# A prefix log-sum-exp: stores on ScalarE's DMA ring, loads on SyncE's, and the last tile in the common stream

## The chip, the cores and the metric

The kernel runs on one core of a Trainium2 chip. The metric is the device time of one execution in microseconds (us): the median of nine runs, and beside it the span and the trace of one profiled execution. Five engines work side by side, each through its own list of instructions in order: TensorE (PE; PEld for its weight loads), VectorE (DVE), ScalarE (ACT), GpSimd (POOL) and SyncE (SP). Transfers between the main memory (DRAM) and the on-chip buffer are done by 16 DMA engines; SyncE or ScalarE issue them with an instruction that returns at once, and a semaphore tells when the transfer has landed.

## The reference

For each batch and each of the 4128 columns, the running log of the sum of exponentials along the 4096 rows:

```python
B, S, D = (4, 4096, 4128)          # x: float32, normal draws
out[:, 0, :] = x[:, 0, :].copy()
for t in range(1, S):
    mx = np.maximum(out[:, t - 1, :], x[:, t, :])
    out[:, t, :] = mx + np.log(np.exp(out[:, t - 1, :] - mx) + np.exp(x[:, t, :] - mx))
```

That is out[t] = log(exp(x[0]) + ... + exp(x[t])), a prefix sum between an exponential and a logarithm. Input and output are 270.5 MB each, so 541 MB have to be moved.

## The kernel before

**Tiles.** The rows of a batch are cut into steps (class `Step`) of 384 rows, three to each of the 128 partitions, which lie one behind the other in DRAM: a partition's share of a full step is one stretch of 3 x 4128 x 4 = 49536 bytes. Ten such steps and one of 256 rows (33024 bytes to a partition) make a batch. In the first batch the short step comes first, in the other three last. So there are 44 steps, numbered 0 to 43; step 0 and step 43 are short. A step's tile `xt` is loaded by one DMA, worked on in place, and stored by one DMA. The pool `xpool` has four buffers (`bufs`).

**Chunks.** A step is worked on in four chunks of columns (class `Chunk`), in the order 3, 0, 1, 2 (`order`); chunk 3 (`firstc`) has 1056 columns, the others 1024. For each chunk: `act(Exp)` on ScalarE; `own` on VectorE adds the partition's own rows, the total going to `tot`; `head` on TensorE puts into PSUM (`above`) the sum of all the partitions above, by a matrix multiplication with a triangle of ones, and for chunk 2 the carry from the step before; `add_above` on VectorE adds that to the rows, and for chunk 2 copies the carry out; `complete` on TensorE leaves the step's total in PSUM for the next step; `act(Ln)` on ScalarE ends it. The last 32 columns of chunk 3 have a small sequence of their own (`tail_head`, `carry_t`).

**The order.** It is written out by hand (`tc.manual_schedule`, lines 196 to 213), and the framework only adds the semaphores. In round g of the loop come: Exp of chunk g+2, `own` and `head` of chunk g+1, `add_above` and `complete` of chunk g, and `result` of chunk g-1, which is its Ln and, behind a step's last chunk (2), the store. So on ScalarE, Exp of three chunks of a step stand ahead of the last Ln of the step before. The loop of line 196 runs twice: over steps 0 to 42 together, and then over step 43 alone, so that the stream of rounds drains between the two.

**The queues.** All loads and stores are issued by SyncE (lines 103 and 106), in program order. The first four loads are issued at the start. Then, in `result`, the store of step k is issued, and right behind it the load of step k+3 (`ahead` is 3; the condition of line 191 begins with step 4). That load goes into the buffer of step k-1, and so it waits until the store of step k-1 has landed. A store waits for the last Ln of its step. As SyncE's list is in order, a waiting store also holds back the load that stands behind it. All transfers go through one queue of the DMA engines (q1 in the profile), as a ring from which each engine takes packets in order: a transfer gives each of the 16 engines 8 packets, one for each of 8 partitions, and a four-byte semaphore write behind them.

**Names in the profile.** L118 is every Exp and Ln (`Chunk.act`), L86 every add, L83 every matrix multiplication, L155 the copies of the carry, L103 a load, L106 a store.

Of the kernel before, what the change touches and what calls it, by code (L numbers as in the profile page):

```python
# [9 lines left out]
ACT = mybir.ActivationFunctionType  # L10
# [28 lines left out]
def kernel(  # L39
# [14 lines left out]
    nc = tc.nc  # L54
# [5 lines left out]
    order = [NC - 1] + list(range(NC - 1))  # L60
    firstc, lastc = order[0], order[-1]
# [5 lines left out]
    bufs = 4  # L67
# [20 lines left out]
    class Step:  # L88
# [14 lines left out]
            nc.sync.dma_start(out=self.xt, in_=self.dram(x))  # L103

        def store(self):
            nc.sync.dma_start(out=self.dram(out), in_=self.xt)  # L106

    class Chunk:
        def __init__(self, step, c):
# [58 lines left out]
    steps = []  # L168
# [9 lines left out]
            row += P * r  # L178
        assert row == S

    ahead = bufs - 1
    for s in steps[:bufs]:
        s.load()
    stored = 0

    def result(k):
        nonlocal stored
        k.act(ACT.Ln)
        if k.c == lastc:
            k.t.store()  # L190
            if bufs <= stored + ahead < len(steps):
                steps[stored + ahead].load()
            stored += 1


    for part in (steps[:-1], steps[-1:]):
        chunks = [Chunk(s, c) for s in part for c in order]
        N = len(chunks)
        for g in range(-2, N + 1):
            if 0 <= g + 2 < N:  # L200
                chunks[g + 2].act(ACT.Exp)
            if 0 <= g + 1 < N:
                chunks[g + 1].own()
                chunks[g + 1].head()
            if 0 <= g < N:
                chunks[g].add_above()
                if g + 1 < N and chunks[g + 1].c == firstc:
                    chunks[g + 1].tail_head()
                chunks[g].complete()
            elif g == -1:  # L210
                chunks[0].tail_head()
            if 0 <= g - 1:
                result(chunks[g - 1])


# [28 lines left out]
```

The softmax here doesn't subtract the row's maximum and nothing guards it: scores larger than these inputs give would overflow.

## Time and profile before

| what | time, us |
|---|---|
| median of nine runs (lowest to highest) | 1265.2 (1264.2 to 1266.37) |
| the profiled execution | 1264.2 |
| its span, from the first to the last instruction | 1262.4 |
| ScalarE (ACT), busy of the span | 921.0 |
| VectorE (DVE), busy of the span | 1024.2 |
| ScalarE waiting for loads, 41 times | 314.9 |
| a full load, from issue to landing (median of 40) | 41.9 |
| a full store, from issue to landing (median of 40) | 27.7 |
| the store of the last step, from issue to landing | 11.1 |

Columns of the views that follow: a timeline's line is start, duration, engine, source line, operation, output and input, number of instructions merged, and in brackets the idle time ahead of it and what ended it. A line of the windows' table is a stretch of time, its length, then busy time and number of instructions by engine, the clock granted to TensorE, the mean busy share of the 16 DMA engines, and what these moved in GB/s. A packet is counted whole in the window in which it starts, so that a share can come out a little over 1. The line of a queue gives its packets, its megabytes, and the time of its packets as a share of 16 engines' span. The trace also holds a record of each packet (start, duration, size, queue, but not which of the 16 engines) and of each engine's share in each landing.

### The profile page before, as it was taken

What the parts mean: (1) busy time and instruction counts of PE and PEld (TensorE: products, weight loads), DVE (VectorE), ACT (ScalarE), POOL (GpSimd) and SP (SyncE); (2) the same over time, 40 slices, a digit from 0 to 9 for tenths busy, and PEclk for the clock granted to TensorE, in tenths of its full rate; (3) what the DMA queues carried; (4) which work ended last, traced back from release to release, by engine and by line L of the source; (5) the groups of instructions that cost most, each with busy time, mean ns of one, the idle gap of its engine ahead of it and who ended that gap; (6) DMA issues with size and microseconds to landing.
All of it is one profiled execution on the core that took longest, in us unless ns stands there. A gap on an engine that the chain in (4) does not pass through costs nothing.

```text
span 1262.4 us, 3545 instructions
## 1 busy us (share of the span) xinstructions
PE 484.1 (38%) x876; PEld 221.4 (18%) x876; DVE 1024.2 (81%) x858; ACT 921.0 (73%) x353; POOL 1.5 (0%) x10
## 2 busy tenths in 40 slices
PE   2445433343334434443324434443332443443332
PEld 1212111111111112211111112211111211111111
DVE  4999878888888888888679888887867988887784
ACT  4986677777777776668669776666966977666784
POOL 0000000000000000000000000000000000000000
PEclk9865656555565555556556565555555656555556
DMA  9999999999999999999999999999999999999997
GB/s 410 413 444 424 427 430 441 432 430 437 432 432 430 440 432 429 433 438 434 435 431 431 432 440 433 427 433 438 426 425 435 429 438 432 433 430 437 435 403 340
DMA packets 12692, 541.29 MB, mean 429 GB/s; under 512 B 1408, under 2 KB 1408, under 8 KB 1408
## 3 DMA queue, kind: packets, MB, share of 16 engines
q1 hardware_dynamic: 12672, 541.07, 99.4%
q8 instruction: 7, 0.11, 0.0%
q14 instruction: 13, 0.11, 0.0%
HBM read 270.53 MB, written 270.53 MB: 429 GB/s over the span
## 4 chain that ended last, share of the span: by engine, by line
DMA 69%; ACT 19%; issue 7%; DVE 3%; SPq 0%; PE 0%; DVEq 0%; ACTq 0%
DMA xt<-in_x_dram 63%; ACT xt L118 19%; DMA out_dram<-xt 6%; DVE xt L86 3%; DVE tot L86 1%; SPq L106 0%; PE above L83 0%; DVE carry L155 0%; DVEq L239 0%; ACTq L118 0%; DVE carry_t L155 0%; DVEq L86 0%
## 5 line engine op out<-in xcount | busy, mean ns | idle before, releaser
L118 ACT ACTIVATE xt<-xt 128x3072 f32<-128x3072 f32 (+3 forms) x352 | 919.7, 2692 | 328.6 <-DMA xt<-in_x_dram 314.9
L83 PE MATMUL above<-tot,excl 128*128 128x512 f32 (+1 forms) x396 | 257.4, 719 | 476.5 <-DVE tot L86 472.2
L86 DVE TENSOR_TENSOR xt<-xt,above 128x2048 f32<-128x2048 f32 (+3 forms) x220 | 393.3, 1788 | 0.0
L86 DVE TENSOR_TENSOR xt<-xt 128x1024 f32<-128x1024 f32 (+1 forms) x160 | 196.9, 1231 | 179.9 <-ACT xt L118 177.5
L86 DVE TENSOR_TENSOR tot<-xt 128x1024 fp32r<-128x1024 f32 (+1 forms) x176 | 217.0, 1233 | 40.5 <-ACT xt L118 18.9
L86 DVE TENSOR_TENSOR xt<-tot,above 128x1024 f32<-128x1024 f32 (+1 forms) x220 | 221.3, 1006 | 0.0
L83 PEld LDWEIGHTS above<-tot,excl 128*128 128x128 f32 x396 | 104.8, 306 | 607.7 <-DVE tot L86 566.5
L83 PE MATMUL above<-tot,rest 128*128 128x512 f32 x240 | 129.5, 635 | 201.8 <-DVE xt L86 201.8
L83 PE MATMUL above<-carry,pick 128*128 128x512 f32 x160 | 141.9, 987 | 0.0
L83 PEld LDWEIGHTS above<-tot,rest 128*128 128x128 f32 x240 | 53.3, 277 | 294.3 <-DVE xt L86 292.5
L83 PE MATMUL above<-carry_t,pick 128*128 128x32 f32 x80 | 25.2, 409 | 83.2 <-DVE xt L86 83.2
L83 PEld LDWEIGHTS above<-carry,pick 128*128 128x128 f32 x160 | 52.0, 325 | 11.3
L83 PEld LDWEIGHTS above<-carry_t,pick 128*128 128x128 f32 x80 | 20.2, 312 | 110.3 <-DVE xt L86 108.3
L155 DVE COPY carry<-xt 32x1024 f32<-32x1024 f32 x40 | 27.6, 691 | 1.4
L155 DVE COPY carry_t<-xt 32x32 f32<-32x32 f32 x40 | 7.1, 177 | 1.4
L63 ACT ACT_TABLE_LOAD x1 | 1.3, 1283 | 0.8 <-PEq L228 0.8
L77 DVE MEMSET carry<- 128x1024 f32 x1 | 0.9, 912 | 1.1 <-PEq L228 1.1
L24 POOL TENSOR_SCALAR_AFFINE_SELECT excl<-excl 128x128 fp32r<-128x128 f32 x1 | 0.3, 293 | 0.0
L24 POOL TENSOR_SCALAR_AFFINE_SELECT pick<-pick 128x128 f32<-128x128 f32 x1 | 0.3, 292 | 0.1
L24 POOL TENSOR_SCALAR_AFFINE_SELECT rest<-rest 128x128 fp32r<-128x128 f32 x1 | 0.3, 292 | 0.0
L23 POOL MEMSET pick<- 128x128 f32 x1 | 0.2, 205 | 0.0
L23 POOL MEMSET excl<- 128x128 f32 x1 | 0.2, 204 | 0.3 <-POOLq L228 0.3
(6 smaller groups left out, 0.7 us busy)
## 6 DMA issues: line engine op xcount, KB each, us to landing
xt<-in_x_dram SPq DMA_DIRECT2D x40, 6192.0 KB, 41.9
out_dram<-xt SPq DMA_DIRECT2D x40, 6192.0 KB, 27.7
xt<-in_x_dram SPq DMA_DIRECT2D x4, 4128.0 KB, 37.0
out_dram<-xt SPq DMA_DIRECT2D x4, 4128.0 KB, 25.4
```

Of the source, the lines that this page charges most:

```text
L23: nc.gpsimd.memset(t.bitcast(FP32), 1.0 - fill)
L24: nc.gpsimd.affine_select(out=t, in_=t, pattern=[[step, P]], compare_op=op, fill=fill, base=base, channel_multiplier=-step if step else 1,)
L63: nc.scalar.preload_act_table_set("natural_log_exp_and_others")
L77: nc.vector.memset(carry, 0.0)
L83: nc.tensor.matmul(o, lhsT=w, rhs=rhs, start=start, stop=True, skip_group_check=True)
L86: nc.vector.tensor_tensor(out=o, in0=a, in1=b, op=mybir.AluOpType.add)
L118: nc.scalar.activation(v, v, func)
L155: nc.vector.tensor_copy(cr[96:, :], t.xt[96:, n, a:b])
```

## The change

Stores are issued by ScalarE, so that they go through a ring of their own. They stand in ScalarE's list right behind the step's last Ln. SyncE's list holds nothing but loads: behind the first four, the load of step k+4 is written behind the store of step k, into the buffer of that same step, and waits until that store has landed. The loop over two parts is gone: step 43 runs in one stream with the steps before it. On ScalarE, three Exp of step 43 now stand ahead of the last Ln of step 42 and its store; on VectorE, `own` of step 43's first chunk stands ahead of `add_above` of step 42's last. Each engine does the same computing instructions in the same number.

```diff
         def store(self):
-            nc.sync.dma_start(out=self.dram(out), in_=self.xt)
+            nc.scalar.dma_start(out=self.dram(out), in_=self.xt)
...
-    ahead = bufs - 1
     for s in steps[:bufs]:
         s.load()
     stored = 0
...
             k.t.store()
-            if bufs <= stored + ahead < len(steps):
-                steps[stored + ahead].load()
+            if stored + bufs < len(steps):
+                steps[stored + bufs].load()
             stored += 1
-
-    for part in (steps[:-1], steps[-1:]):
-        chunks = [Chunk(s, c) for s in part for c in order]
-        N = len(chunks)
-        for g in range(-2, N + 1):
...
+    chunks = [Chunk(s, c) for s in steps for c in order]
+    N = len(chunks)
+    for g in range(-2, N + 1):
+        if g + 2 < N:
+            chunks[g + 2].act(ACT.Exp)
+        if 0 <= g + 1 < N:
+            chunks[g + 1].own()
+            chunks[g + 1].head()
+        if 0 <= g < N:
+            chunks[g].add_above()
+            if g + 1 < N and chunks[g + 1].c == firstc:
+                chunks[g + 1].tail_head()
+            chunks[g].complete()
+        elif g == -1:
+            chunks[0].tail_head()
+        if 0 <= g - 1:
+            result(chunks[g - 1])
```

More of the change, by code (lines that the diff above doesn't have):

```diff
@@ L190, in result @@
             k.t.store()
-            if bufs <= stored + ahead < len(steps):
-                steps[stored + ahead].load()
+            if stored + bufs < len(steps):
+                steps[stored + bufs].load()
             stored += 1
-    for part in (steps[:-1], steps[-1:]):
-        chunks = [Chunk(s, c) for s in part for c in order]
-        N = len(chunks)
-        for g in range(-2, N + 1):
[L200 to L213, printed above, removed]
+    chunks = [Chunk(s, c) for s in steps for c in order]
[15 more added lines that the diff above has]
+            result(chunks[g - 1])
 _INS = ['x']
```

## The prediction

> **What bounds the kernel now.** I read the head of the page first (busy time, the span in slices, the queues).
>
> ```profile
> span 1262.4 us, 3545 instructions
> ...
> PE 484.1 (38%) x876; PEld 221.4 (18%) x876; DVE 1024.2 (81%) x858; ACT 921.0 (73%) x353; POOL 1.5 (0%) x10
> ...
> DMA  9999999999999999999999999999999999999997
> ...
> q1 hardware_dynamic: 12672, 541.07, 99.4%
> q8 instruction: 7, 0.11, 0.0%
> q14 instruction: 13, 0.11, 0.0%
> ```
>
> No compute engine is full. The 16 DMA engines are, in all slices but the last, and nearly all of it is one queue, q1, that carries loads and stores. The packet records say at what rate: a full-length packet of 49536 B takes 1829 ns (median, 10,240 of them), one of 33024 B takes 1222 ns (1,024). The difference, 607 ns for 16512 B, is 27.2 GB/s; what is left of each is a fixed 8 ns. Each engine carries 704 packets, 640 x 1.829 + 64 x 1.222 = 1248.8 us: of a span of 1262.4 only 13.6 us are anything else. Is there room inside? Three stretches of two tiles each, by engine:
>
> ```profile
> core 0: us, PE busy (x) PEld busy (x) DVE busy (x) ACT busy (x) POOL busy (x), PEclk, DMA share, GB/s
> 300.00:359.00 59.00, 20.05 (x35) 8.77 (x35) 47.53 (x40) 42.99 (x16) 0.00 (x0) 0.50 1.00 432
> 359.00:418.00 59.00, 23.07 (x44) 10.79 (x44) 48.66 (x41) 43.00 (x16) 0.00 (x0) 0.59 1.00 434
> 418.00:477.00 59.00, 23.88 (x44) 11.10 (x43) 48.81 (x41) 43.00 (x16) 0.00 (x0) 0.56 1.00 433
> ```
>
> The DMA share is 1.00; ScalarE works 21.5 and VectorE 24.3 us of each tile's 29.3. So only the end is left, where the last slice shows a 7. There the timeline of ScalarE, that of SyncE's queue, and two windows with the columns of the table above:
>
> ```profile
> 1197.11 21.50 ACT L118 ACTIVATE xt<-xt 128x3168 f32<-128x3168 f32 x8 [7.75 <-DMA xt<-in_x_dram]
> 1218.94 2.76 ACT L118 ACTIVATE xt<-xt 128x3072 f32<-128x3072 f32 x1 [0.34 <-DVE xt L86]
> 1224.81 2.76 ACT L118 ACTIVATE xt<-xt 128x3072 f32<-128x3072 f32 x1 [3.10 <-DVE xt L86]
> 1228.86 10.02 ACT L118 ACTIVATE xt<-xt 128x3072 f32<-128x3072 f32 x5 [1.29 <-DVE carry L155]
> ```
>
> ```profile
> 1184.38 0.42 SPq L103 DMA_DIRECT2D xt<-in_x_dram  x1
> 1213.24 37.55 SPq L106 DMA_DIRECT2D out_dram<-xt  x3
> ```
>
> ```profile
> 1229.00:1232.00 3.00, 0.00 (x0) 0.00 (x0) 0.00 (x0) 3.00 (x2) 0.00 (x0) 0.50 0.23 99
> 1247.00:1251.00 4.00, 0.00 (x0) 0.00 (x0) 1.43 (x2) 3.09 (x2) 0.00 (x0) 0.93 0.03 12
> ```
>
> The second-to-last tile (number 42) drains with three waits on VectorE; only then does the last tile (43) get its Exp, although its load was issued at 1184.38 and landed 37.1 us later, at 1221.5. The engines stand nearly idle twice, before store 42 (issued 1231.65) and before store 43 (1250.46). That looks like 3 + 4 us to be had. It is not, because a transfer lands when the slowest of 16 engines is done. By the records of landings, store 41 was finished on the fastest engine at 1229.1 and on the slowest at 1236.1; this lag grew from 0.6 us at the start, with a step of about 1 us at most of the instruction fetches that fell on that engine. On it there is no first gap: store 42 was queued before 1236.1 and landed at 1250.7, and store 43's packets began at 1251.3. Its landing mark lies 0.35 us behind its last packet, so it stood idle for about 0.9 us. That is all the end can give.
>
> **The change, part by part.** *Stores leave SyncE's queue (44 issues).* On it each load (k+3) stood behind store k, and the stores waited for ScalarE for 1194.3 us in all; the loads did so with them. Afterwards load k+4 waits for store k to land. In steady state, with both rings filled and taken in turn, each transfer takes 29.3 us instead of 14.6. From the landing of load k+1, store k is issued 16.1 us later (six activations; 1137.70 to 1153.84), lands 29.3 + 1.2 after that, at 46.6, and load k+4 is issued there; but load k+3 keeps its ring filled until 2 x 29.3 = 58.6. The slack is 12 us for stores that queue up, and when the loads' ring does run dry, the stores have the engines alone and catch up. The order of the work changes, not its amount: 0 us. If both rings ran dry at each tile, landing and issue would lie open, 1.2 x 40 = 48 us.
>
> *ScalarE issues the stores.* The row for one is 0.33 us, with 0.05 of waiting around it; the far bound is the dearest single thing in ScalarE's rows that is no activation, the table load at 1.28. So 0.4 to 1.3 us a tile. Behind it stand the next tile's fourth Exp, then the Ln of its first chunk; VectorE waits for that Exp. Cover: ScalarE's 7.75 us of waiting for a load in each tile, and VectorE's 177.5 / 40 = 4.4 us of waiting for ScalarE behind it. Price 0; without that cover it would be 44 x 0.4 = 18 us.
>
> *Start.* Loads 0 to 3 are issued as before. Store 0 (41.28) no longer stands behind load 3: 8 packets of each alternate, 8 x 3.05 = 24.4, from 42.2 to 66.6. Load 3 then lands at 67 instead of 57.9. It is needed two activations after store 1 (63.71 + 5.4 = 69.1). Hidden, with 2 us to spare. Load 4 is issued when store 0 lands, 67 against 67.72.
>
> *One queue or two: the price of a ring change.* Before, an engine changes between load and store once in 8 packets; afterwards at almost every packet, 704 - 88 = 616 times more. What a change of direction costs is shown: the first packet behind a transfer's semaphore write is 2 ns over its norm between 200 and 1200 us, other packets 4 ns, so nothing. A change of ring is shown by the 20 fetches only. Each sits between two packets of q1 without a gap, and the next packet runs long: 0.41 us on average behind the 8 KB fetches (0.12 to 0.66), 0.44 behind the 16 KB ones. Taken as the price of a change that is 616 x 0.41 = 253 us, the upper bound. But fetch and lengthening together are 0.32 + 0.41 = 0.72 us for 8 KB and 1.02 + 0.44 = 1.45 us for 16 KB: twice the bytes, twice the time, and nothing left over for the change itself. From below, the 8 ns of fixed price could be what two rings hide: 704 x 8 ns = -5.6 us. I take 0, nearest to the two-size rows, and keep -5.6 and the small positive prices for the range.
>
> A rule of the Trainium skill ("DMA: Bandwidth & Descriptors", section "Issuing engines are not separate DMA queues") says that transfers from several issuing engines end up on the same 16 DMA engines, interleaved, and that only issue time is saved. The page on trace analysis ("Perfetto Trace Analysis", "DMA Optimizations") advises the contrary, one issuing engine for inputs and another for outputs, where control flow needs more freedom. By the first the two rings bring nothing; by the second they free loads from waiting behind stores, which the share of 1.00 says nobody is short of.
>
> *The last tile streamed.* The slowest engine has 44 loads and 42 stores done at 1235.8 in either order, as it never rests. Store 42 now comes behind three Exp of tile 43, and these wait for load 43 (1221.5; ScalarE is free at 1218.6): 3 x 1.93 + 3 x 2.75 less small overlaps = 13.6, so 1235.1, plus 0.25 for wait and issue, plus 0.85 from issue to first packet (1250.46 to 1251.30) = 1236.2. It is issued 3.7 us later than before and leaves a gap of 0.4 on the slowest engine. Store 42 then runs 14.7, to 1250.9. Store 43: behind store 42's issue come Exp 1.9 and four Ln of 1.93, 1235.4 + 0.4 + 9.6 = 1245.4. VectorE has five adds of 1.2 left behind that Exp (1237.6), so it is done at 1243.6, as ScalarE comes to the last Ln. The packets are queued by 1246.3, and the second gap closes. 1250.9 + 8 x 1.231 + 0.35 = 1261.1, against 1250.46 + 11.1 = 1261.57: -0.5 us. If load 43 lands later by x, store 42 does too, and x is paid, less what store 42 does not need. I allow 3 us for it.
>
> Sum: 0 + 0 + 0 + 0 - 0.5. The span goes to 1261.9; this execution took 1264.2 us with a span of 1262.4, so 1263.7; the median of the nine runs is 1.0 above this execution: **1264.7 us**.
>
> **Rivals.** *A ring change has a price* (slower). Place: between any two packets of a DMA engine. If the fixed 8 ns are paid again, 616 x 8 = 4.9 us, 1269.6; 25 ns would be 15.4, 1280. It decides from (1267.7 - 1264.7) / 616 = 5 ns. For it: packets behind a fetch do run long, and all 16 engines are saturated, so any price shows in full. Against it: the two sizes of fetch, and the free changes of direction.
>
> *Two rings hide the fixed 8 ns* (faster): 1264.7 - 5.6 = 1259.1. For it: two sources of the next packet. Against it: on one ring packets already follow each other without a gap that I can see.
>
> *The last loads come late* (slower). Alternation at the end holds load 43 back behind store 41, store 42 is late by the same, and the slowest engine waits for it, 3 us or more: 1268 to 1270. Against it: load 43 has only two thirds of the bytes, and store 41 starts 16 us after load 42.
>
> *The rings don't interleave*: whichever is served first, the engines stay busy, for each ring holds a transfer ahead. Same time as the forecast.
>
> **How the numbers follow.** A measurement of this kernel can tell about 0.2% from no change, 2.5 us: 1262.7 to 1267.7. The forecast, with the unserved interleaving, has 0.43 and that as its own range. The price of a ring change has 0.33, late last loads 0.08, together 0.41 slower; the hidden fixed price 0.16, faster. The range reaches down to the faster rival, 1259, and up to a ring change of 25 ns, 1280; left out are dearer changes and little else.
>
> **What would show it.** Right: q1 and a second hardware queue with about 49.7% each and 99.4% together; packets still 1829 ns; loads some 32 us and stores 30 to 41 us to landing; ScalarE's wait for loads near 300 us; store 43 issued before store 42 has landed. Wrong by the first rival: longer packets or gaps, and less than 433 GB/s in the middle, where nothing but the rings has changed. Wrong by the third: a dip of the DMA share before store 42 of more than the 0.23 window above. A share under 0.99 in the middle would overthrow the claim that one ring always covers the other.

## The result, and the profile after

The changed kernel takes 1274.17 us (median of 10 executions, 1269.63 to 1281.78), the kernel before 1264.84 (31 executions beside it, 1263.43 to 1266.37): a ratio of 1.0078, with a 95% interval of 1.0067 to 1.0089. It is slower by 0.8%, some 9.3 us. Its profiled execution took 1269.48 us with a span of 1267.8, which is 4.7 below its median; so the trace shows 5.4 us of loss, and what the median loses beyond that can be seen only in the traces of slower executions, e1 and e3 below. (Ratios here leave out an execution that is over 1.5% above its kernel's fastest, medians and ranges don't; that matters for e5, e11 and e15 below.)

The head of the page of the changed kernel, with the rows that answer to those of before:

```profile
span 1267.8 us, 3412 instructions
...
PE 484.6 (38%) x876; PEld 221.5 (17%) x876; DVE 1024.6 (81%) x858; ACT 925.3 (73%) x353; POOL 1.5 (0%) x10
...
DMA  9999999999999999999999999999999999999997
GB/s 408 423 425 430 429 444 428 430 439 427 436 435 428 438 433 424 442 430 387 433 427 433 427 444 427 428 443 429 408 434 429 430 436 437 430 436 432 430 414 337
...
q1 hardware_dynamic: 6336, 270.54, 49.7%
q10 hardware_dynamic: 6336, 270.54, 49.5%
```

The same GB/s row of the page of before, which was not shown there:

```profile
GB/s 410 413 444 424 427 430 441 432 430 437 432 432 430 440 432 429 433 438 434 435 431 431 432 440 433 427 433 438 426 425 435 429 438 432 433 430 437 435 403 340
```

The queues are as forecast, two with half of the packets each, and the compute engines are as busy as they were, within 0.5%. The row of digits hides the loss, because a 9 is anything from 0.9 up. The GB/s row shows it: slices of 31.7 us with 387 and 408 stand among some 430, the 19th and the 29th, where before has 434 and 426. The windows' table tells more. First the three stretches that the prediction looked at, then the one around the 19th slice, in the changed kernel:

```profile
300.00:359.00 59.00, 16.82 (x31) 7.18 (x30) 47.36 (x40) 43.39 (x17) 0.00 (x0) 0.53 1.00 431
359.00:418.00 59.00, 22.93 (x42) 10.58 (x42) 47.99 (x41) 42.85 (x17) 0.00 (x0) 0.59 1.00 434
418.00:477.00 59.00, 23.34 (x42) 10.75 (x42) 48.41 (x42) 43.27 (x17) 0.00 (x0) 0.56 1.01 435
...
585.00:590.00 5.00, 1.22 (x2) 0.50 (x2) 4.97 (x4) 5.00 (x3) 0.00 (x0) 0.50 0.80 343
590.00:595.00 5.00, 2.44 (x4) 1.00 (x4) 4.83 (x7) 4.58 (x3) 0.00 (x0) 0.50 0.81 347
595.00:600.00 5.00, 3.46 (x6) 1.99 (x7) 4.82 (x5) 4.46 (x3) 0.00 (x0) 0.50 0.98 317
```

The last three of these windows in before:

```profile
585.00:590.00 5.00, 2.39 (x4) 0.94 (x4) 4.83 (x6) 5.00 (x3) 0.00 (x0) 0.50 0.99 426
590.00:595.00 5.00, 3.70 (x6) 2.02 (x7) 4.82 (x5) 2.19 (x2) 0.00 (x0) 0.50 1.03 446
595.00:600.00 5.00, 2.44 (x7) 0.99 (x5) 4.13 (x4) 5.00 (x3) 0.00 (x0) 0.84 1.03 446
```

In the steady stretches share and GB/s are those of before (1.00; 432, 434, 433): two rings taken in turn carry as much as one. Around 590 the share falls to 0.80, so some engines stand idle. Then, from 595 to 600, the share is back at 0.98 but only 317 GB/s go through: the engines are busy with packets that take longer. These are two different losses, and both are small in place and time.

What happens there, by the records of issues and landings (an ordinary listing from the trace; "first" and "last" are the fastest and the slowest of the 16 engines; S is a store, L a load, and step 21 is one of the short ones):

```
      issue    first    last
L20  537.36   564.30   574.65
S18  561.86   585.31   592.88
L21  567.35   588.97   597.22
S19  590.88   618.83   624.95
L22  592.93   626.16   628.63
```

Load 20 lands when its slowest engine is done, 10.35 us after its fastest. The six activations behind it start then, and store 19 is issued 16.2 us later, at 590.88. Load 22 has to wait for store 18, and that for its slowest engine, at 592.88. But the fastest engines had ended store 18 at 585.3 and load 21 at 589.0. By these records an engine that had ended both had nothing in either ring until the packets of store 19 arrived, and the share of 0.80 fits.

Second, the end. ScalarE's timeline of the changed kernel, and the windows ahead of store 42:

```profile
1203.27 16.11 ACT L118 ACTIVATE xt<-xt 128x3168 f32<-128x3168 f32 x6 [7.19 <-DMA xt<-in_x_dram]
1219.41 0.34 ACTq L106 DMA_DIRECT2D out_dram<-xt  x1
1219.79 5.50 ACT L118 ACTIVATE xt<-xt 128x3072 f32<-128x3072 f32 x2 [0.41 <-ACT xt L118]
1227.61 13.53 ACT L118 ACTIVATE xt<-xt 128x2112 f32<-128x2112 f32 x6 [2.31 <-DMA xt<-in_x_dram]
1241.16 0.34 ACTq L106 DMA_DIRECT2D out_dram<-xt  x1
...
1253.11 0.34 ACTq L106 DMA_DIRECT2D out_dram<-xt  x1
```

```profile
1236.00:1239.00 3.00, 1.44 (x5) 1.22 (x5) 2.94 (x4) 3.00 (x3) 0.00 (x0) 0.50 0.08 33
1239.00:1242.00 3.00, 0.60 (x2) 0.00 (x0) 2.90 (x5) 2.58 (x2) 0.00 (x0) 0.50 0.00 0
```

Load 43 landed at 1227.5 instead of 1221.5, so store 42 is issued at 1241.16, behind 6 us with a share of 0.08 and 0.00. The slowest engine ended store 41 at 1239.9 (before: 1235.8) and got the first packet of store 42 at 1242.0. Store 43 is issued before store 42 has landed (1257.2), as forecast, and lands at 1266.9, against 1261.6 before. The loss of this execution is thus 4.1 us until the slowest engine has ended store 41, and 2.1 us of gap behind it where before had 0.9 in all: 5.3 of the 5.4 us.

Averaged over the 16 engines, the time in packets of tiles and the rest of the span (idle, and a little for semaphore writes and fetches) are, in us:

```
                       span    packets   rest
before                1262.4    1253.5    8.9
changed               1267.8    1256.7   11.1
changed, again (e3)   1269.7    1258.1   11.6
rings alone (e1)      1273.7    1260.0   13.7
tail alone (e2)       1260.9    1253.1    7.8
```

More than half of what is lost is longer packets. That looks like the first rival, a price of a ring change; the sections that follow show that it isn't.

### The profile page after: what moved, and what is told of

It is laid out like the page before. It is cut to its first block, busy times and chain, and to the rows that moved or that the text cites. A ratio compares the mean times of both kernels' runs of the same rounds, so it can differ in the third digit from the quotient of the medians.

```text
span 1267.8 us, 3412 instructions
## 1 busy us (share of the span) xinstructions
PE 484.6 (38%) x876; PEld 221.5 (17%) x876; DVE 1024.6 (81%) x858; ACT 925.3 (73%) x353; POOL 1.5 (0%) x10
## 4 chain that ended last, share of the span: by engine, by line
DMA 73%; ACT 17%; DVE 7%; issue 1%; PE 1%; DVEq 0%; ACTq 0%; SPq 0%
DMA xt<-in_x_dram 41%; DMA out_dram<-xt 32%; ACT xt L118 17%; DVE xt L86 5%; DVE tot L86 2%; PE above L83 1%; DVE carry L155 0%; DVEq L236 0%; ACTq L106 0%; SPq L103 0%; DVE carry_t L155 0%; ACTq L118 0%; DVEq L86 0%
## 5 line engine op out<-in xcount | busy, mean ns | idle before, releaser
L83 PEld LDWEIGHTS above<-carry,pick 128*128 128x128 f32 x160 | 52.2, 326 | 11.3
## 6 DMA issues: line engine op xcount, KB each, us to landing
out_dram<-xt ACTq DMA_DIRECT2D x40, 6192.0 KB, 35.4
```

Source lines behind the costliest of these rows:

```text
L83: nc.tensor.matmul(o, lhsT=w, rhs=rhs, start=start, stop=True, skip_group_check=True)
```

## The experiments

Theories under test, with the letters that the expectations use where they use any: C, both directions in flight at once cost bandwidth; D1, the loads' ring runs dry, because the drift between the 16 engines eats the slack of 12 us; D2, the short steps cause it; D3, the traffic of the compute engines does. The expectations of e1 to e5 name the first theories, R, T and D, in their own words; D1 to D3 are D worked out further. The "margin" of a load below is the time from its issue to the fastest engine's end of the load ahead of it in the ring; with less than 1 us it is "late", as about that long passes between issue and first packet.

**Which part of the change costs (e1, e2, e3).** The rings alone, in the kernel before (e1, the first edit); the streamed tail alone (e2, the second); the changed kernel once more on the same chip (e3).

```diff
-            nc.sync.dma_start(out=self.dram(out), in_=self.xt)
+            nc.scalar.dma_start(out=self.dram(out), in_=self.xt)
```

```diff
-    for part in (steps[:-1], steps[-1:]):
+    for part in (steps,):
```

> Only the ring of the stores is changed against the kernel before (stores issued by ScalarE); the last tile keeps its own pass. Theory R (two rings make the 16 engines drift apart and packets run long; the loss is in the middle): about as slow as the changed kernel, 1271 to 1276 us, ratio 1.005 to 1.009, and a wide scatter of several us. Theory T (the loss is the last tile's late load, which the streamed tail turns into a late store): no loss, 1264 to 1266.

> Only the last tile's separate pass is taken away; all transfers stay on SyncE's ring in the order of the kernel before. Theory R: -0.5 us as the prediction worked out, so 1264 to 1265, narrow scatter. Theory T: slower, 1270 or more. In the profile: store 42 issued near 1235 on the span, store 43 near 1245.5, and a single gap before store 42 on the slowest engine of less than 1 us.

> The changed kernel once more, for a second trace of a usual execution (the first one traced, 1269.5 us, was the fastest of its 11). Theory R: packets still 1829 ns by the median, but in one or two stretches many packets on both rings 0.5 to 1.5 us over their norm, and the slowest engine done with store 41 some 4 to 10 us later than the 1236 us of the kernel before. Theory T: the slowest engine is done with store 41 at 1236 to 1240 and the rest of the loss stands as a gap before store 42.

e1: 1275.51 us (1269.17 to 1280.88), ratio 1.0078 (1.0054 to 1.0102). e2: 1263.48 (1262.44 to 1264.63), ratio 0.9986 (0.9978 to 0.9995). e3: 1273.35 (1269.89 to 1282.43), ratio 1.0075 (1.0049 to 1.0101). The whole loss comes with the rings, as theory R had it: 10.2 us between e1 and before, 9.9 between e3 and e2. In e3's trace store 41 lands at 1242.2, 6.1 us later than before. The streamed tail by itself gains 1.8 us, and e2 is faster than both kernels. ScalarE's timeline of e2 at the end has a wait of 2.92 us for load 43, and then two of 1.54 and 1.20 for VectorE:

```profile
1220.73 18.98 ACT L118 ACTIVATE xt<-xt 128x2112 f32<-128x2112 f32 x9 [2.92 <-DMA xt<-in_x_dram]
1241.25 1.91 ACT L118 ACTIVATE xt<-xt 128x2048 f32<-128x2048 f32 x1 [1.54 <-DVE xt L86]
1244.36 1.91 ACT L118 ACTIVATE xt<-xt 128x2048 f32<-128x2048 f32 x1 [1.20 <-DVE xt L86]
```

Store 42 is issued at 1234.28 and store 43 at 1246.29; the end is 1260.03. In e1, with the tail in a pass of its own, two windows are empty, one ahead of store 42 and one ahead of store 43:

```profile
1239.00:1242.00 3.00, 0.00 (x0) 0.00 (x0) 0.00 (x0) 2.53 (x2) 0.00 (x0) 0.52 0.08 33
...
1258.00:1262.00 4.00, 0.00 (x0) 0.00 (x0) 1.73 (x2) 2.54 (x2) 0.00 (x0) 0.50 0.00 0
```

With two rings the streamed tail closes the second of them.

**Is it the ring change, or two directions at once (e4, e5)?** The chunks are taken out and each tile is stored as it was loaded, through one ring (e4) and through two (e5, with the line of e1).

```diff
-    for part in (steps[:-1], steps[-1:]):
...
+    for s in steps:
+        s.store()
+        if bufs <= stored + ahead < len(steps):
+            steps[stored + ahead].load()
+        stored += 1
```

> All arithmetic is left out: each tile is loaded and stored as it is, so that the output is the input; all transfers on SyncE's ring, in the order of the kernel before. The DMA work is that of the kernel before, 1248.8 us of packets at their norm, with nothing late at the end but the last stores. Both theories: 1254 to 1262 us, narrow scatter, long packets (200 ns over the norm) about as many as the 81 of the kernel before or fewer.

> The same copy with the stores on ScalarE's ring. Theory C (loads and stores in flight at once make packets run long, whatever the engines do): slower than the copy on one ring by 3 to 10 us, wide scatter, 150 long packets or more. Theory D (only the wait of a store for compute lets both rings run dry and then start all 16 engines together): no compute, stores never late, so within 2 us of the copy on one ring and about as few long packets.

One ring: 1258.66 us (1258.29 to 1259.43), ratio 0.9955 (0.9940 to 0.9970). Two: 1261.24 (1254.99 to 1304.17), ratio 0.9971 (0.9954 to 0.9987). The two intervals overlap, and in the profiled execution of e5 the packets are as short as anywhere: 41 of the 10,240 full ones are over 200 ns above their norm, against 60 in e4 and 81 in before. Here the engines change rings at five of six packets and have both directions in flight all the time, with a median margin of 48.6 us. (A packet's record doesn't name its engine; each engine's packets are followed here by time, every one starting where another ended.) So in this trace neither costs what the changed kernel loses. The times alone are less clear: the medians differ by 2.6 us, between the 2 that D had as its bound and the 3 that C had as its least, and the scatter is wide, as C had it (nine executions at 1255.0 to 1265.2, one at 1304.2). That scatter is not explained; e7, below, speaks against C as well.

**More slack, in the real kernel (e6 to e9).** With two rows to a partition instead of three, tiles are two thirds as large. Six buffers give the rings more in store (e6 one ring, e7 two), four give less than before (e8 one ring, e9 two). All have the streamed tail. The edit of e6 and e7 (e8 and e9 have its first half):

```diff
-R = 3
+R = 2
...
-    bufs = 4
+    bufs = 6
```

> The kernel of one ring and streamed tail with all steps of 256 rows (64 alike, no short ones) and six buffers in the same space. Packets of 33024 B: 1024 to an engine x 1.222 = 1251.3 us at the norm, 2.5 more than before. Both theories: 1263 to 1270 us, narrow scatter.

> The same with the stores on ScalarE's ring. Theory C: slower than its one-ring partner by 5 to 12 us, as with the large tiles. Theory D: a store comes after two thirds of the time and there are no short steps at which both rings run dry, so no loss, within 2.5 us of its partner, and no dips in the row of GB/s in the middle of the span.

> All steps of 256 rows as in the pair before, but four buffers instead of six, all on SyncE's ring. In the ring's order a store has to be issued some 11 us after a landing and is wanted after 19.5: both theories 1265 to 1272 us.

> The same with the stores on ScalarE's ring. By the steps of the prediction a load is issued about 31.7 us after a landing and the ring of the loads is empty at 39: 7 us of slack, where the engines drift 10 us apart. Theory D1 (too few buffers ahead: the loads' ring runs empty on the fast engines before the store has landed on the slowest): slower than its one-ring partner by 3 us or more, long packets all over the span. Theory D2 (the short steps are what does it, since there the slack falls by 9.8 us): no short steps, so within 2.5 us of the partner.

e6: 1266.63 us (1264.99 to 1267.17), ratio 1.0012 (1.0003 to 1.0022); e7: 1264.58 (1264.30 to 1266.85), ratio 1.0005 (0.9996 to 1.0015). With slack, two rings cost nothing, where C had forecast 5 to 12 us. In e7 the engines drift as far apart as in the changed kernel (the median store lands 9.4 us after its fastest engine, against 8.5), but the median margin is 13.5 us and no load is late. Its GB/s row has no dip between start and end:

```profile
GB/s 401 420 432 433 434 434 433 434 434 433 431 432 433 435 432 430 429 434 434 434 433 434 434 434 432 433 431 431 435 432 429 434 433 433 434 434 434 434 427 285
```

e8: 1286.05 (1280.34 to 1290.56), ratio 1.0182 (1.0155 to 1.0209); e9: 1282.62 (1279.81 to 1282.85), ratio 1.0138 (1.0123 to 1.0153). With less slack both lose, the one ring too, although by its records only 2 of 61 stores find its engines without work; the median store is issued 2.2 us before the fastest engine has ended what is queued ahead of it (8.0 in before). Both have long packets in number: 354 and 349, against 86 and 69 in e6 and e7. Between e6 and e8 only the number of buffers differs, so the loss is one of too little queued work, and two rings are one way to get there. Three forecasts missed here: e8 was to take 1265 to 1272 us, and e9 was to be 3 us or more slower than e8 by D1, or within 2.5 us of it by D2. It was 3.4 us faster, though 55 of its 59 loads are late. Why the second ring should help there is not explained. With these tiles, then, no pair shows a loss that comes with the second ring; that slack decides is seen at the size of the real tiles in e5, e13 and e15.

**Without the short steps (e10, e11).** The last 256 rows of each batch are left out, which leaves 40 full steps; e10 has one ring, e11 two, both the streamed tail.

```diff
-        parts = [R] * (n // R) + ([n % R] if n % R else [])
+        parts = [R] * (n // R)
```

> The last 256 rows of every batch are left out (neither loaded, computed nor stored), so that there are 40 full steps and no short ones; four buffers of 384 rows, one ring. DMA work 80 x 8 x 1.829 = 1170.6 us; both theories: 1182 to 1192 us.

> The same without the last 256 rows, stores on ScalarE's ring. Theory D1: the slack of 12 us is used up by the drift without any short step, the loads' ring is empty on the fast engines at most steps, so still 4 us or more slower than the one-ring partner. Theory D2: without the short steps no loss, within 2.5 us of the partner, and no dip in the row of GB/s.

e10: 1189.46 us (1189.35 to 1189.59), ratio to before 0.9406. e11: 1210.83 (1192.68 to 1219.01), ratio 0.9494 (0.9422 to 0.9566). Without short steps the loss of two rings is still there, and scatters more (by the medians it is 1.8%; the ratio of e11 rests on its two fastest executions). D2 falls as the cause. e11 also shows best how longer packets look in the windows' table, in an early and in a late stretch:

```profile
150.00:400.00 250.00, 92.61 (x167) 42.06 (x167) 206.27 (x172) 186.51 (x71) 0.00 (x0) 0.55 1.00 434
800.00:1100.00 300.00, 109.23 (x198) 49.80 (x198) 239.24 (x197) 214.35 (x80) 0.00 (x0) 0.57 1.00 421
```

The late stretch in e10:

```profile
800.00:1100.00 300.00, 111.31 (x202) 50.76 (x202) 247.30 (x206) 221.59 (x83) 0.00 (x0) 0.57 1.00 433
```

The share is 1.00 in both stretches of e11, so the engines hardly rest, but late in the run 3% fewer bytes go through in the same busy time. Early in e11 the engines take load and store mostly in strict turn, about 800 packets of each kind, and a packet between two of the other ring is less than 2 ns over its norm: the alternation is free. In the whole run 26 of 35 loads are late, with a median margin of -3.3 us; in the late stretch all of them are, with margins of -4.4 to -5.1 us, and the regular turns are lost.

**Earlier stores, or none of the arithmetic (e12 to e15).** e12 and e13 leave Exp and Ln out, on one ring and on two, so that a store is ready some 10 us sooner after its load. e14 and e15 are the copy again, with no arithmetic on the tiles, but with each store delayed as in the real kernel: it waits for the next tile's load, and then for 14 activations on a scratch tile. The two edits:

```diff
-            v = self.t.xt[:, :, self.a:self.b]
-            nc.scalar.activation(v, v, func)
+            pass
```

```diff
+    for k, s in enumerate(steps):
+        if k + 1 < len(steps):
+            wait_on(steps[k + 1].xt[:, 0, 0:1])
+        for _ in range(14):
+            nc.scalar.activation(scr_b, scr_a, ACT.Exp)
+        wait_on(s.xt[:, 0, 0:1])
+        s.store()
```

> Exp and Ln are left out: the sums run on the raw numbers, so that the output is not the reference's; same transfers, buffers, adds and matrix multiplications, streamed tail, one ring. All theories: the packets' 1248.8 us and some 10 to 14 more, 1258 to 1264 us.

> The same without Exp and Ln, stores on ScalarE's ring. A store then is issued some 6 us after the landing of the next load instead of 16, so the loads' ring has some 22 us of slack. Theory D1 (the loads' ring runs empty on the fast engines, and packets after that run long): no loss, within 2.5 us of the one-ring partner, no load issued after its ring is empty, under 100 long packets. Theory D3 (two streams and the compute engines' traffic in the same tiles collide): VectorE's traffic is all there, so still 4 us or more slower, 130 long packets or more.

> The copy without arithmetic on the tiles (output is the input), but each store waits for the next tile's load and for about 16 us of activations on a scratch tile, as the stores of the real kernel wait for their Ln; one ring. Theories D1 and D3: as the plain copy on one ring or a little more, 1258 to 1264 us, under 100 long packets.

> The same delayed copy with the stores on ScalarE's ring. Theory D1: the wait alone brings the loss back, 4 us or more slower than the one-ring partner, wide scatter, loads issued after their ring is empty at 20 steps or more, 130 long packets or more. Theory D3: no arithmetic on the tiles, so no loss, within 2.5 us of the partner.

e12: 1262.65 us (1261.48 to 1263.61), ratio 0.9981 (0.9972 to 0.9991). e13: 1266.74 (1261.05 to 1271.99), ratio 1.0015 (0.9994 to 1.0037). Stores come 6.1 us after the next load's landing instead of 16.2; late loads go down from 25 to 6 of 39, and the loss of two rings from about 10 to 4 us. D1 had forecast no loss, no late load and under 100 long packets, and missed all three (there are 120 long ones); the 4 us are what D3 had as its least. So this pair doesn't decide between them: a median margin of 5.7 us is not enough for all of 39 loads.

e14: 1262.00 (1261.37 to 1262.71), ratio 0.9978 (0.9968 to 0.9988). e15: 1281.74 (1266.08 to 1287.48), ratio 1.0081 (1.0037 to 1.0124). Against e5, only the delay of the stores is added, with the activations that make it, which e14 has as well; and the loss is back, with 21 of 39 loads late. VectorE and TensorE work on no tile here, while e7, with all of the kernel's arithmetic, loses nothing: D3 falls, and the delay is what matters. The profiled execution of e15 was one of its fastest (1268.26), so its trace holds only a part of the loss, and 124 long packets where D1 had looked for 130 or more.

**All pairs.** Late loads and margins (us) are those of the two-ring kernel; "long" is the number of full packets over 200 ns above the norm, one ring and two, in the profiled execution; the ratios are to the kernel before.

```
pair                      late     margin   long         one ring  two rings
e4/e5   copy              0/39     48.6      60 ->  41    0.9955    0.9971
e6/e7   R 2, 6 buffers    0/59     13.5      86 ->  69    1.0012    1.0005
e12/e13 no Exp, no Ln     6/39      5.7      64 -> 120    0.9981    1.0015
e14/e15 copy, delayed    21/39      0.5      57 -> 124    0.9978    1.0081
e2/e3   the kernel       29/39      0.4      78 -> 214    0.9986    1.0075
e10/e11 no short steps   26/35     -3.3     129 -> 379    0.9406    0.9494
e8/e9   R 2, 4 buffers   55/59     -1.5     354 -> 349    1.0182    1.0138
```

Where no load is late, two rings cost at most 0.2%; where half of them are, about 1%, unless the one ring is short of work already.

Where in time the longer packets lie is one more reading: the time above the norm, in us for an average engine, in each 100 us from the start.

```
               0   100  200  300  400  500  600  700  800  900 1000 1100 1200
before        1.8  0.7  0.2  0.1  0.1  0.1  0.1  0.1  0.2  0.9  0.1  0.1  0.2
changed       2.5  0.1  0.1  0.2  0.3  1.6  0.6  0.3  0.2  1.7  0.1  0.1  0.3
e1            2.4  0.3  0.3  0.6  0.9  1.9  2.1  0.1  0.1  1.9  0.2  0.1  0.4
e7            1.8  0.1  0.1  0.1  0.1  0.1  0.1  0.1  0.1  0.1  0.1  0.1  0.2
e15           1.6  0.1  0.0  0.1  0.1  0.3  1.5  0.0  0.0  1.7  0.4  0.1  0.2
e11           3.7  0.5  0.1  0.2  0.1  0.4  0.8  1.3  1.7  3.6  3.6  0.5  0.0
```

In the changed kernel they come in bursts near 600 and 910, just behind the short steps 21 and 32, whose loads fill the ring for a third less time; in e15 near 640 to 690 and 900 to 920. Before has a small one near 900 too. e11, without short steps, has them late: its loads are late from 370 us on, but up to 600 us this costs under 0.5 us in each 100; more than half comes between 800 and 1100, where the margins are -4.4 to -5.1 us. Loads that were 2 to 3 us late cost little there.

## Why the prediction was wrong, step by step

**The step that failed** is the first of the change: "The slack is 12 us for stores that queue up, and when the loads' ring does run dry, the stores have the engines alone and catch up. The order of the work changes, not its amount: 0 us". The 12 us were worked out as if the 16 engines were one. In the changed kernel the median margin of a load is 0.55 us, not 12, and 25 of 39 loads are late. The term that was put at 0 measured 9.9 us (e3 against e2). Both ends moved. The store took 35.5 us from issue to landing (median) where the step had 30.5, as it lands with its slowest engine, 8.5 us behind the fastest: the next load's issue comes 5.0 us later. And the fastest engine ends a load 4.3 us before the landing that the step counted with (the median spread of a load). That is 9.3 of the 11.5 us; the other 2 are not traced to one cause. The prediction had the drift in hand, "this lag grew from 0.6 us at the start", and used it at the end of the run alone. On one ring the drift is harmless: each engine has the next load queued behind the store, whatever the others do (in before a load is issued a median of 22 us before the fastest engine has ended what lies ahead). With two rings taken in turn the spread grew from at most 7.4 us to 11 or 12.

**"When the loads' ring does run dry, the stores have the engines alone and catch up"** failed too. Around 590 the stores' ring is then nearly empty as well, the share falls to 0.80, and the packets that follow are long. The test was named in advance: "A share under 0.99 in the middle would overthrow the claim that one ring always covers the other". That was met, at 585 to 595.

**Rival one, a price of a ring change**, gave the right sign and a time of the right size, 1269.6 to 1280, for a wrong reason. In the changed kernel 91.8% of the full packets take 1829 ns to the nanosecond (85.4% before), and e5 and e7 change rings more often (about 590 and 690 times an engine, against 490) and lose 0.2% or nothing. The step that set this price to 0 was right; its count of changes, at almost every one of 704 packets, was too high. Rival two, the hidden 8 ns, is refuted by the same 1829.

**Rival three, late last loads**, came true as a consequence: load 43 landed 6 us late, store 42 was issued at 1241.16 instead of 1235.4, and the dip ahead of it went below the 0.23 window. By itself it is worth the 2.1 us of gap, where before has 0.9; the argument against it, that "load 43 has only two thirds of the bytes", did not count the dry rings before.

**ScalarE issues the stores**: right. A store costs it 0.41 us between two activations, 0.34 of that for the issue, and this came out of its waiting for loads, which stays near 300 us. The first two lines of ScalarE's table of waits in the changed kernel (total, times, longest):

```profile
ACT xt L118 <- DMA xt<-in_x_dram: 303.1, 42, 14.4
ACT xt L118 <- ACT xt L118: 17.9, 43, 0.5
```

**The start**: right. Load 3 landed at 66.33 (67 forecast), load 4 was issued at 68.02 (67 forecast; 67.72 in before), and nothing waited for it.

**The streamed tail**: the mechanism was right, the size too small: -0.5 us forecast, -1.8 measured in e2 (ratio 0.9986, 0.9978 to 0.9995). In e2's profiled execution store 42 was issued at 1234.28 (1235.4 forecast) and the end came at 1260.03 (1261.1). One reading was off: VectorE was to be done as ScalarE comes to the last Ln, but ScalarE waited for it twice (1.54 and 1.20), so store 43 came 12.0 us behind store 42 instead of 10.0. It cost nothing, because store 42 landed only at 1250.28. Load 43 landed 0.8 us earlier than in the trace of before, which the change doesn't account for.

The Trainium skill ("DMA: Bandwidth & Descriptors", "Queues, rings and completion order") says that each engine serves the rings that have work in turn, a packet at a time; the regular alternation early in e11 agrees. The same page's rule that several issuing engines save only issue time ("Issuing engines are not separate DMA queues") fits that nothing was gained here, and says nothing of a loss. What another page suggests, an issuing engine each for inputs and outputs ("Perfetto Trace Analysis", "DMA Optimizations"), cost 0.8% here, and nothing where the loads had 13 us in hand (e7).

What stays open is why packets run long after the rings have run nearly dry. That the two go together is seen in six of the seven pairs and in their place in time; in the seventh, e8 and e9, packets are long on one ring as on two. The mechanism in the DMA engines is not shown by any record here, and no run isolated it.

## What to carry to other kernels

In this kernel, bound by its transfers, moving stores to a second ring brought no bandwidth, and the store that each load waits for took longer to land (35.4 us instead of 27.7). Work out the slack of a queue from the slowest DMA engine's landing to the fastest engine's end: here a median of 5.7 us left 6 of 39 loads late (e13), and 13.5 us none (e7). Where the GB/s of a slice fall while the digits of the DMA row stay at 9, look at share and GB/s together in short windows: a low share is an empty queue, a full share with fewer bytes is longer packets.

## What the runs showed that was not expected

- Packets get longer when queued work is short, on one ring as on two. In the late stretch of e11 the first store packet behind two load packets is about 440 ns above its norm (mean of some 160), and the first load packet behind two stores about 190 ns; strictly alternating packets in the same stretch are up to some 30 ns above it. Early in the same execution the store packet behind two loads is 1 to 3 ns above. So it is not the change of direction as such.
- Kernels of the large tiles whose loads come late scatter by 10 us and more between executions (1269.6 to 1281.8 for the changed one, 1192.7 to 1219.0 for e11), while the one-ring kernels e2, e4, e6, e10, e12 and e14 stay within 0.2 to 2.2 us, and before within 2 to 5. Two kernels don't fit: e5 scatters without a late load, and e9, with nearly all of them late, stays within 3.0 us.
- The drift between DMA engines, 0.6 us at the start and 7.4 at the end in before, reached 11.3 in the changed kernel, 12.3 in e3, 17.2 in e13 and 15.0 in e15. It also reached 13.0 in e7 and 14.3 in e5, which have no late load: drift costs where the slack doesn't cover it.
